# One layer of a GLA and Fourier diffusion backbone: a place of its own for a quarter of the folded h, fewer adaLN steps at GLA's end, slab products and turns in one run

## The chip, the cores and the metric

The kernel runs on one core of one Trainium2 chip. The metric is device time in microseconds of one execution, taken as the median of several runs. TensorE (PE) multiplies matrices, VectorE (DVE) and ScalarE (ACT) work on elements, GpSimd (POOL) fills and adds a little, and SyncE (SP) hands transfers to the DMA queue, in order. Each engine works through its own list of instructions and waits on counts that the others raise.

## The reference

One layer works on 384 tokens (128 of context, 256 latent) of width 2048, in fp32. Cut to what the change touches:

```python
mod = jax.nn.silu(cond) @ lw['w_ada'] + lw['b_ada']
sh1, sc1, ga1, sh2, sc2, ga2 = [m[:, None, :] for m in jnp.split(mod, N_MOD, axis=-1)]
h = rmsnorm(x, lw['norm_pre_mix']) * (1.0 + sc1) + sh1
m, s_f, s_b = mixer(h, s0_f, s0_b, n_chunks, lw)
x = x + ga1 * rmsnorm(m, lw['norm_post_mix'])
h = rmsnorm(x, lw['norm_pre_ffn']) * (1.0 + sc2) + sh2
ff = (jax.nn.silu(h @ lw['w_ffn_gate']) * (h @ lw['w_ffn_up'])) @ lw['w_ffn_down']
```

`cond` is one vector for latent and one for context tokens, so that `mod` has six parts (adaLN) of 2048 channels by 2. The mixer projects h with `w_in` into q, k, v, output gate, low-rank decay factors and Fourier channels; it runs a chunked gated linear attention (GLA) in both directions, a 2-D DFT over tokens and channels of each Fourier group, and merges the two with sigmoid gates `h @ w_gate`; `w_out` follows, and then a dense feed-forward layer.

## The kernel before, in words

All activations lie turned: 128 channels on the partitions, 384 tokens along the free dimension, 16 such tiles (`KT`). An fp32 product is made of three matmuls of a rounded part and a remainder of each factor (`passes`: A_hi with whi, A_hi with wlo, A_lo with whi). ACT rounds a raw weight tile to whi (L256, and L394 for the narrow tile of w_x), DVE subtracts to get wlo (L257, L395). For h they are A_hi (ACT, L331) and A_lo (DVE, L332).

**First stage** (loop from L521 over the 16 channel tiles). For tile kb, `gemv(kb)` multiplies silu(cond) with a 2 MB slab of w_ada (two 1 MB transfers, 16 fp32 matmuls per tile) into columns 0 to 255 of a PSUM tile `pgm`; ACT copies them (`ev`, L562), two PE transposes turn them into columns 256 to 511 of the same tile (L568), DVE reduces these (L575) to shift and scale (`mods`, L576 and L580) and applies them to the normalised x, which gives h (`scr`, L582). From h come A_hi and A_lo. The projection to v runs one tile behind: `vprod(kb - 1)` in three runs of six matmuls (pv, L462). Two further projections (`xprod`, px, L480) and, every fourth tile, the low-rank product of four tiles (`lrprod`, px, L487) share one PSUM tile `px`; after each of them DVE adds px to its sum (`flush`, L475), before the next may start. `todo` holds these px products of an iteration in order: the first runs ahead of the turns, the second behind them, the third behind the second run of pv, the fourth at the end. DVE's subtractions for the next weights (`lag`) come behind A_lo, and then the parts of h's fold for the Fourier branch (`fold_h`, L424 and L426). SP's queue carries slabs (pool of five 1 MB tiles), raw tiles of w_v and xraw tiles of w_x (two of each). The folded h is written to DRAM (`hf_d`).

**adaLN's other blocks.** The five half blocks of parts 2, 3, 4 are formed on DVE by a generator, two half steps of adacc (L664) per 512 KB of weights. `meted` takes as many of them per step of the main loop as `rate` says; while GLA runs, its generator `gla()` yields that number at each of its own steps, and 2 is used once it has ended. A finished block is brought together on PE (pr, L674), copied by ACT (L638) and turned (ptm, L642). The half block left over is made on PE (`ada_pe`, pr from adax, L699) in the stage of `w_out`, where the rest of the DVE generator is used up at tile 12.

**Fold.** Behind GLA the folded h is read back in four quarters (`fetch`, L983) into the two buffers of `fx`. For each quarter `parts_of` makes four fp32 matmuls (bnp, L999), whose weights wn DVE forms once (L992), and splits the quarter into xe and xo. `xo` takes the place of the tiles B_hi and B_lo. The quarters run as steps between the units of the gates.

Of the kernel before, what the change touches and what calls it, by code (L numbers as in the profile page):

```python
# [11 lines left out]
F32 = mybir.dt.float32  # L12
# [11 lines left out]
KT = D // P  # L24
# [83 lines left out]
def tile_step(ctx: ExitStack, tc: tile.TileContext, a, o):  # L108
    nc = tc.nc
    PE, ACT, DVE, POOL, SP = nc.tensor, nc.scalar, nc.vector, nc.gpsimd, nc.sync  # L110
# [34 lines left out]
    def alloc_r(t, name):  # L145
        return tuple(actp.tile([P, 8, T], F32R, tag=f"{t}_{n}", name=f"{name}_{n}") for n in ("hi", "lo"))
# [183 lines left out]
    def split_act(hi, lo, src):  # L330
        ACT.copy(hi, src)  # L331
        DVE.tensor_sub(lo, src, hi.bitcast(F32))  # L332
# [28 lines left out]
    hf_d = dram.tile([P, KT, T], F32, name="hf_d")  # L361
# [3 lines left out]
    with ExitStack() as s:  # L365
# [6 lines left out]
        def load_slab(kb):  # L372
            slabs[kb] = [pb.tile([P, KT // 2, 256], F32, tag="slab", name="slab", bufs=5) for _ in range(2)]
            for n, sl in enumerate(slabs[kb]):
                SP.dma_start(sl, a["w_ada1"][kb, :, n * (KT // 2) : (n + 1) * (KT // 2), :])
# [3 lines left out]
        def load_w(kb):  # L379
            load()  # L380
            xraw[kb] = pb.tile([P, XU * P], F32, tag="xraw", name="xraw", bufs=2)
            SP.dma_start(xraw[kb], a["w_x"][kb])
# [47 lines left out]
        def keep_h(q):  # L430
            (ACT if q else SP).dma_start(hf_d[:, 8 * q : 8 * q + 8, :], xnt[q])
# [9 lines left out]
        def gemv(kb, ks=range(KT)):  # L441
            slab = slabs[kb]
            for k in ks:
                q = 32 * (k % 4)
                PE.matmul(  # L445
                    pgv[q : q + 32, :], spad[:, k, :], slab[k // (KT // 2)][:, k % (KT // 2), :],
                    start=k < 4, stop=k >= KT - 4,
                )

        def passes(w):  # L450
            return ((0, w[0]), (0, w[1]), (1, w[0]))
# [19 lines left out]
        def flush(acc, first, dst=None):  # L471
            if first:
                DVE.tensor_copy(acc, px)
            else:
                DVE.tensor_add(dst if dst is not None else acc, acc, px)  # L475

        def xprod(u, kb, w):
            def mm():
                for j, (x_, w_) in enumerate(passes(w)):
                    PE.matmul(px, w_[:, u * P : (u + 1) * P], hT[x_][:, kb, :], start=j == 0, stop=j == 2)  # L480

            return mm, lambda dst=None: flush(xacc[u], kb == 0, dst)

        def lrprod(kb):
            def mm():
                for q in range(4):
                    PE.matmul(  # L487
                        px[32 * q : 32 * q + 32, :], wlr[:, kb + q, :], scr[:, (kb + q) % 8, :], start=True, stop=True,
                    )

            return mm, lambda dst=None: flush(lracc, kb == 0, dst)
# [30 lines left out]
        prev = None  # L522
        for kb in range(KT):
            if kb and kb + 1 < KT:
                load_slab(kb + 1)
                load_w(kb + 1)
                if kb == 4:
                    load_later()

            if kb == KT - 1:  # L530
                load()
                pre = pb.tile([P, KT // 2, 256], F32, tag="slab", name="pre", bufs=5).rearrange("p a b -> p (a b)")
                for n in range(2):
                    load(pre[:, G * n : G * n + G])
            wait = kb in (1, 2)
            if kb and not wait:
                gemv(kb)
            todo = []
            if kb > 4 and kb % 4 == 2:
                todo.append(lrprod(kb - 6))  # L540
            if kb:
                todo += [xprod(u, kb - 1, prev[1]) for u in range(XU)]
            todo += [None] * (4 - len(todo))
            flushes = [t[1] if t else lambda: None for t in todo]

            def pe_x(n):
                if todo[n]:
                    todo[n][0]()

            if wait:  # L550
                vprod(kb - 1, prev[0], (0,))
            pe_x(0)
            hf = scr[:, kb % 8, :]

            xr = hf if kb else qs[0]
            DVE.tensor_mul(xr, xn(kb), rstd if kb else px)
            flushes[0]()
            if wait:
                gemv(kb)
            if kb:  # L560
                ev = pb.tile([P, 256], F32, tag="ev", name="ev")
                ACT.copy(ev, pgv)  # L562
            lag = []
            new = split_w(kb, lag)
            if kb:
                vprod(kb - 1, prev[0], (1 if wait else 0,))
            for m in range(2):
                PE.transpose(pmod[:, m, :], ev[:, m * P : (m + 1) * P], ident)  # L568
            pm = pb.tile([P, 2, 2], F32, tag="pm", name="pm")
            if kb == 0:  # L570

                for _ in range(6):
                    PE.matmul(pv[5][:, 0:P], ones, ones, start=True, stop=True)
            pe_x(1)
            DVE.tensor_reduce(pm, bands, axis=mybir.AxisListType.X, op=ALU.add)  # L575
            DVE.tensor_scalar(  # L576
                mods[:, 1, kb, :], pm[:, 1, :], bsc1[:, 0, kb : kb + 1], norms[:, 0, kb : kb + 1],
                op0=ALU.add, op1=ALU.mult,
            )
            DVE.tensor_scalar_add(mods[:, 0, kb, :], pm[:, 0, :], cols[:, 0, kb : kb + 1])  # L580
            for lo, hi, c in segs:
                DVE.tensor_scalar(  # L582
                    hf[:, lo:hi], xr[:, lo:hi], mods[:, 1, kb, c : c + 1], mods[:, 0, kb, c : c + 1],
                    op0=ALU.mult, op1=ALU.add,
                )
                if kb == 0:
                    ACT.activation(
                        hT[0][:, kb, lo:hi], xr[:, lo:hi], AF.Identity,
                        bias=mods[:, 0, kb, c : c + 1], scale=mods[:, 1, kb, c : c + 1],
                    )  # L590
            flushes[1]()
            if kb:
                split_act(hT[0][:, kb, :], hT[1][:, kb, :], hf)
            else:
                ACT.copy(rstd, px)
                DVE.tensor_sub(hT[1][:, kb, :], hf, hT[0][:, kb, :].bitcast(F32))
            if kb:
                if not wait:
                    vprod(kb - 1, prev[0], (1,))
                pe_x(2)  # L600
                flushes[2]()
            for sub in lag:
                sub()
            fold_h(kb)
            if kb == KT - 2:
                keep_h(0)
            if kb:
                vprod(kb - 1, prev[0], (2,))
                pe_x(3)
                flushes[3]()  # L610
            prev = new
# [97 lines left out]
    def on(t, h):  # L709

        return qk[:, h:8:4, t * P : (t + 1) * P]
# [16 lines left out]
    with ExitStack() as s:  # L728
# [9 lines left out]
        for c in range(2):  # L738
            src = a["a2"][:, 512 * c : 512 * c + 512]
# [17 lines left out]
        def gla():  # L757
# [10 lines left out]
            for h in range(NH):  # L768
# [129 lines left out]
                for d in range(2):  # L898
                    for n in range(2):
                        t = n * (1 + d)  # L900
# [26 lines left out]
            for t in range(3):  # L927
                for h in range(NH):
                    z = on(t, h)
                    ACT.mul(z, z, rs[:, t, h : h + 1])  # L930
                yield 2

        def keep(t, i):
            return lambda p: ACT.copy(t[:, i, :], p)
# [34 lines left out]
    with ExitStack() as s:  # L969
# [9 lines left out]
        fold_in.append(pxe)  # L979
        fx = actp.tile([P, 2, 4, T], F32, tag="C_lo", name="fx")  # L980

        def fetch(b):
            SP.dma_start(fx[:, b % 2], hf_d[:, 4 * b : 4 * b + 4, :])  # L983

        fetch(0)
        fetch(1)
        xe = pxe.tile([P, KT, 2, HT], F32R, name="xe")
        xo = alloc_r("B", "xo")
        wn4 = pxe.tile([P, G], F32, tag="ws", name="wn4")[:, 0 : 32 * KT].rearrange("p (k c) -> p k c", c=32)
        POOL.memset(wn4, 0.0)  # L990
        w01 = wnr.rearrange("p (g i) k -> p i k g", i=2)
# [2 lines left out]

        def parts_of(b):

            src = fx[:, b % 2]
            for q in range(4):
                PE.matmul(  # L999
                    bnp[32 * q : 32 * q + 32, :], wn4[:, 4 * b + q, :], src[:, q, 0:HT], start=b == 0, stop=b == 3,  # L1000
                )
            e = xe[:, 4 * b : 4 * b + 4]
            split_act(e[:, :, 0], e[:, :, 1], src[:, :, 0:HT])
            d = xo[b // 2][:, 4 * (b % 2) : 4 * (b % 2) + 4]
            split_act(d[:, :, 0:HO], d[:, :, HO : 2 * HO], src[:, :, HT:T])
            if b < 2:
                fetch(b + 2)

        def folding():
            for b in range(4):  # L1010
# [228 lines left out]
    with ExitStack() as s:  # L1239
# [675 lines left out]
        for kind, c, i in steps:  # L1915
# [14 lines left out]
            if kind == "D":  # L1930
                w = grab2()
                n, kh = i // 2, i % 2
                if kh == 0:
# [8 lines left out]
                todo = [  # L1942
                    (pd_tiles[t], [[x[:, 2 * kh + m, t * P : (t + 1) * P] for m in range(2)] for x in h], mov_d, kh == 0, kh == 1)
                    for t in ts
                ]
# [24 lines left out]
            elif kind[0] == "D":  # L1970
# [3 lines left out]
                todo = []  # L1974
# [8 lines left out]
            else:  # L1983
# [4 lines left out]
                B = banks(c)  # L1988
# [232 lines left out]
```

## Time and profile before

| | |
|---|---|
| time, median of 3 runs | 1919.46 us (1918.77 to 1920.14) |
| profiled execution, time | 1918.24 us |
| profiled execution, span | 1916.5 us |
| TensorE clock granted, mean | 0.999 |
| PE busy | 1894.8 us (99%) |
| DVE busy | 1637.8 us (85%) |
| ACT busy | 1081.0 us (56%) |
| DMA moved | 435.65 MB, mean 227 GB/s |

The profile is of one execution; the span is from its first to its last instruction, and its time has what lies around these besides. In a row of a timeline stand start, duration, engine, line, operation, out<-in and shape, the count of instructions, and in square brackets the idle time just before it with what ended that. A duration counts until the result is there, so that successive matmuls overlap; the rate of PE is read from one start to the next. PEld are weight loads, which run beside the matmuls. SPq and PEq are the queues' own instructions.

### The profile page before, as it was taken

Reading aid. Unit: us, or ns where it says so; the run is one execution under the profiler, and the core shown is the slowest. Engines: PE = TensorE matmul, PEld = TensorE weight load, DVE = VectorE, ACT = ScalarE, POOL = GpSimd, SP = SyncE. Lnnn points to the kernel's source line nnn. Section 1 sums busy time; section 2 is a strip of 40 time slices with the busy share of each in tenths; the row PEclk is TensorE's granted clock in tenths of the full one; section 3 lists DMA queues with packets and bytes.
Section 4 is the critical chain, followed back from the end, with each engine's and each line's share of the span. In section 5 each row is a group of like instructions: output and inputs, shape, how many; then the busy total and the mean of one; then the engine's idle time right before and its main releaser. Section 6 shows DMA issues by size and latency. Waiting matters only on the chain.

```text
span 1916.5 us, 27971 instructions
## 1 busy us (share of the span) xinstructions
PE 1894.8 (99%) x10364; PEld 1669.1 (87%) x10364; DVE 1637.8 (85%) x2120; ACT 1081.0 (56%) x1569; POOL 160.8 (8%) x189
## 2 busy tenths in 40 slices
PE   8999999999999999999999999999999999999997
PEld 5779999999999999999988888888888888888886
DVE  6777989787867897877799999999999999988985
ACT  4335545554447554446457666766676666666554
POOL 0000001000000000004000111111102021111001
PEclk9999999999999999999999999999999999999999
DMA  9986777786765788766449697888879696959563
GB/s 390 376 328 201 236 236 229 237 281 207 228 193 189 259 272 286 285 216 217 145 144 273 167 250 185 240 205 222 214 209 240 183 249 175 270 126 271 135 221 101
DMA packets 247385, 435.65 MB, mean 227 GB/s; under 512 B 45772, under 2 KB 150412, under 8 KB 242640
## 3 DMA queue, kind: packets, MB, share of 16 engines
q1 hardware_dynamic: 199648, 391.59, 60.8%
q0 software_dynamic: 18944, 33.63, 11.5%
q10 hardware_dynamic: 28656, 8.65, 2.5%
q8 instruction: 81, 1.33, 0.3%
q14 instruction: 56, 0.46, 0.1%
HBM read 369.05 MB, written 57.67 MB: 223 GB/s over the span
## 4 chain that ended last, share of the span: by engine, by line
PE 85%; DVE 6%; DMA 4%; ACT 2%; issue 1%; SPq 0%; DVEq 0%; ACTq 0%
PE pgu L1737 31%; PE pmm L291 25%; PE pdn L1737 10%; PE pds L1737 7%; PE pv L462 3%; DVE wlo L257 1%; PE pfo L1100 1%; PE pgm L445 1%; DVE adacc L664 1%; PE pmm L1451 1%; ACT whi L256 1%; PE px L480 1%; PE pfo L1101 1%; PE bk L1737 1%; DMA xraw<-in_w_x 1%
## 5 line engine op out<-in xcount | busy, mean ns | idle before, releaser
L291 PE MATMUL pmm<-A_hi,whi 128*128 128x384 f32 x1072 | 361.9, 338 | 0.0
L291 PE MATMUL pmm<-A_lo,whi 128*128 128x384 f32 x1072 | 358.7, 335 | 0.0
L291 PE MATMUL pmm<-A_hi,wlo 128*128 128x384 f32 x1072 | 358.7, 335 | 0.0
L1635 ACT CAST whi<-u 128x1024 fp32r<-128x1024 f32 x200 | 210.7, 1055 | 174.7 <-PE pgu L1737 40.9
L1646 DVE TENSOR_TENSOR wlo<-u,whi 128x1024 fp32r<-128x1024 f32 x200 | 244.2, 1223 | 34.8 <-ACT whi L1635 30.4
L256 ACT CAST whi<-raw 128x1024 fp32r<-128x1024 f32 x163 | 171.1, 1053 | 158.2 <-DMA raw<-in_w_out 59.0
L1737 PE MATMUL pgu<-whi,A_hi 128*128 128x512 f32 x640 | 249.9, 390 | 0.0
L1737 PE MATMUL pgu<-whi,A_lo 128*128 128x512 f32 x640 | 249.1, 389 | 0.0
L257 DVE TENSOR_TENSOR wlo<-raw,whi 128x1024 fp32r<-128x1024 f32 x161 | 196.1, 1221 | 42.4 <-ACT whi L256 41.7
L1635 ACT CAST whi<-raw 128x1024 fp32r<-128x1024 f32 x157 | 165.2, 1054 | 84.9 <-PE pgu L1737 25.3
L291 PEld LDWEIGHTS pmm<-A_hi,whi 128*128 128x128 f32 x1072 | 201.2, 188 | 5.5 <-issue 4.1
L291 PEld LDWEIGHTS pmm<-A_lo,whi 128*128 128x128 f32 x1072 | 201.4, 188 | 0.5 <-DVE A_lo L332 0.2
L291 PEld LDWEIGHTS pmm<-A_hi,wlo 128*128 128x128 f32 x1072 | 201.2, 188 | 0.0
L1646 DVE TENSOR_TENSOR wlo<-raw,whi 128x1024 fp32r<-128x1024 f32 x157 | 191.8, 1222 | 11.0 <-ACT whi L1635 10.5
L664 DVE SCALAR_TENSOR_TENSOR adacc<-adaw,cond,adacc 128x1024 f32<-128x1024 f32 x150 | 186.8, 1281 | 14.5 <-DMA adaw<-in_w_ada 14.2
L1737 PE MATMUL pgu<-wlo,A_hi 128*128 128x512 f32 x640 | 185.8, 389 | 0.0
L1737 PEld LDWEIGHTS pgu<-whi,A_hi 128*128 128x128 f32 x640 | 120.1, 188 | 25.9 <-issue 0.8
L1737 PEld LDWEIGHTS pgu<-wlo,A_hi 128*128 128x128 f32 x640 | 120.1, 188 | 25.1
L1737 PEld LDWEIGHTS pgu<-whi,A_lo 128*128 128x128 f32 x640 | 120.1, 188 | 24.8
L1737 PE MATMUL pgu<-whi,S 128*128 128x512 f32 x400 | 116.6, 389 | 0.0
L1870 POOL DMA_DIRECT2D sums_d<-spare x64 | 58.5, 954 | 622.6 <-ACT spare L1866 601.4
L1737 PE MATMUL pdn<-whi,hid_hi 128*128 128x512 f32 x264 | 102.8, 389 | 0.0
(466 smaller groups left out, 3536.1 us busy)
## 6 DMA issues: line engine op xcount, KB each, us to landing
adaw<-in_w_ada SPq DMA_DIRECT2D x80, 512.0 KB, 4.6
raw<-in_w_d SPq DMA_DIRECT2D x70, 512.0 KB, 6.0
slab<-in_w_ada SPq DMA_DIRECT2D x32, 1024.0 KB, 11.3
raw<-in_w_gate SPq DMA_DIRECT2D x64, 512.0 KB, 4.3
raw<-in_w_g SPq DMA_DIRECT2D x48, 512.0 KB, 3.8
raw<-in_w_u SPq DMA_DIRECT2D x48, 512.0 KB, 5.1
u<-in_w_u SPq DMA_DIRECT2D x40, 512.0 KB, 5.5
u<-in_w_g SPq DMA_DIRECT2D x40, 512.0 KB, 9.5
```

What stands on the lines that cost most here:

```text
L256: ACT.copy(hi, raw)
L257: sub = lambda: eng.tensor_sub(lo, raw, hi.bitcast(F32))
L291: PE.matmul(dst, w[wi][:, k * n + n0 : k * n + n0 + P], x[xi][:, k0 + k, :], start=first and k == 0 and j == 0, stop=last and k == kts - 1 ...
L445: PE.matmul(pgv[q : q + 32, :], spad[:, k, :], slab[k // (KT // 2)][:, k % (KT // 2), :], start=k < 4, stop=k >= KT - 4,)
L462: PE.matmul(pv[2 * t + g], hT[x_][:, kb, t * P : (t + 1) * P], w_[:, g * 512 : (g + 1) * 512], start=kb == 0 and j == 0, stop=kb == KT - 1 ...
L480: PE.matmul(px, w_[:, u * P : (u + 1) * P], hT[x_][:, kb, :], start=j == 0, stop=j == 2)
L664: DVE.scalar_tensor_tensor(acc[:, c, :], w, cond[:, k, c : c + 1], acc[:, c, :], op0=ALU.mult, op1=ALU.add,)
L1100: PE.matmul(p, w[0][:, c], x[:, 0 : 2 * n], start=kh == k == 0, stop=False)
L1635: ACT.copy(hi, src)
L1646: DVE.tensor_sub(lo, src, hi.bitcast(F32))
L1737: PE.matmul(dst, stat[x_][m], mov(w[w_], m), start=first and w_ == m == x_ == 0, stop=last and w_ == m == 1, skip_group_check=any(more),)
L1870: POOL.dma_start(sums_d[k], u, accum_op=ALU.add)
```

## The change

It has three parts.

In the first stage, `joined` holds for tiles 6 to 15. There `gemv(kb + 1)` is written right behind the two turns of tile kb; gemv(6) stays at the head of its iteration. The low-rank product of a joined tile is put second in `todo` instead of first. From tile 6 on a slab is asked for one tile earlier than the w tiles: slab 8 behind gemv(7), slab 9 ahead of w 8, and so on.

In GLA, the last three steps yield 2, 1 and 0 instead of 2, 2 and 2.

In the fold, quarter 2 goes into the half of `xo` that takes the place of B_lo's channels 4 to 7, and is asked for together with quarters 0 and 1; quarter 3 goes into `fx[:, 0]` and is asked for behind part 0.

```diff
--- before.py
+++ after.py
@@ -522,7 +522,10 @@
         prev = None
         for kb in range(KT):
             if kb and kb + 1 < KT:
-                load_slab(kb + 1)
+                if kb < 7:
+                    load_slab(kb + 1)
+                elif kb + 2 < KT:
+                    load_slab(kb + 2)
                 load_w(kb + 1)
                 if kb == 4:
                     load_later()
@@ -533,13 +536,17 @@
                 for n in range(2):
                     load(pre[:, G * n : G * n + G])
             wait = kb in (1, 2)
-            if kb and not wait:
+            joined = kb > 5
+            if kb and not wait and kb < 7:
                 gemv(kb)
             todo = []
-            if kb > 4 and kb % 4 == 2:
+            low = kb > 4 and kb % 4 == 2
+            if low and not joined:
                 todo.append(lrprod(kb - 6))
             if kb:
                 todo += [xprod(u, kb - 1, prev[1]) for u in range(XU)]
+            if low and joined:
+                todo.insert(1, lrprod(kb - 6))
             todo += [None] * (4 - len(todo))
             flushes = [t[1] if t else lambda: None for t in todo]
 
@@ -566,6 +573,10 @@
                 vprod(kb - 1, prev[0], (1 if wait else 0,))
             for m in range(2):
                 PE.transpose(pmod[:, m, :], ev[:, m * P : (m + 1) * P], ident)
+            if joined and kb < KT - 1:
+                gemv(kb + 1)
+                if kb == 6:
+                    load_slab(kb + 2)
             pm = pb.tile([P, 2, 2], F32, tag="pm", name="pm")
             if kb == 0:
 
@@ -928,7 +939,7 @@
                 for h in range(NH):
                     z = on(t, h)
                     ACT.mul(z, z, rs[:, t, h : h + 1])
-                yield 2
+                yield 2 - t
 
         def keep(t, i):
             return lambda p: ACT.copy(t[:, i, :], p)
@@ -979,13 +990,15 @@
         fold_in.append(pxe)
         fx = actp.tile([P, 2, 4, T], F32, tag="C_lo", name="fx")
 
+        xo = alloc_r("B", "xo")
+        folded = [fx[:, 0], fx[:, 1], xo[1][:, 4:8, :].bitcast(F32), fx[:, 0]]
+
         def fetch(b):
-            SP.dma_start(fx[:, b % 2], hf_d[:, 4 * b : 4 * b + 4, :])
-
-        fetch(0)
-        fetch(1)
+            SP.dma_start(folded[b], hf_d[:, 4 * b : 4 * b + 4, :])
+
+        for b in range(3):
+            fetch(b)
         xe = pxe.tile([P, KT, 2, HT], F32R, name="xe")
-        xo = alloc_r("B", "xo")
         wn4 = pxe.tile([P, G], F32, tag="ws", name="wn4")[:, 0 : 32 * KT].rearrange("p (k c) -> p k c", c=32)
         POOL.memset(wn4, 0.0)
         w01 = wnr.rearrange("p (g i) k -> p i k g", i=2)
@@ -994,7 +1007,7 @@
 
         def parts_of(b):
 
-            src = fx[:, b % 2]
+            src = folded[b]
             for q in range(4):
                 PE.matmul(
                     bnp[32 * q : 32 * q + 32, :], wn4[:, 4 * b + q, :], src[:, q, 0:HT], start=b == 0, stop=b == 3,
@@ -1003,8 +1016,8 @@
             split_act(e[:, :, 0], e[:, :, 1], src[:, :, 0:HT])
             d = xo[b // 2][:, 4 * (b % 2) : 4 * (b % 2) + 4]
             split_act(d[:, :, 0:HO], d[:, :, HO : 2 * HO], src[:, :, HT:T])
-            if b < 2:
-                fetch(b + 2)
+            if b == 0:
+                fetch(3)
 
         def folding():
             for b in range(4):
```

On PE, in the first stage round tile 8 (pgm from slab are the slab products, pgm from ident the turns), this stood before, from one tile's slab products to the next's:

```order
L445 MATMUL pgm<-slab,spad 32x256 x16
L480 MATMUL px<-A_hi,whi 128x384
L480 MATMUL px<-A_hi,wlo 128x384
L480 MATMUL px<-A_lo,whi 128x384
L462 MATMUL pv<-whi,A_hi 128x512 x6
L568 MATMUL pgm<-ident,ev 128x128 x2
L480 MATMUL px<-A_hi,whi 128x384
L480 MATMUL px<-A_hi,wlo 128x384
L480 MATMUL px<-A_lo,whi 128x384
L462 MATMUL pv<-wlo,A_hi 128x512 x6
L462 MATMUL pv<-whi,A_lo 128x512 x6
```

After the change it reads:

```order
L480 MATMUL px<-A_hi,whi 128x384
L480 MATMUL px<-A_hi,wlo 128x384
L480 MATMUL px<-A_lo,whi 128x384
L462 MATMUL pv<-whi,A_hi 128x512 x6
L575 MATMUL pgm<-ident,ev 128x128 x2
L445 MATMUL pgm<-slab,spad 32x256 x16
L480 MATMUL px<-A_hi,whi 128x384
L480 MATMUL px<-A_hi,wlo 128x384
L480 MATMUL px<-A_lo,whi 128x384
L462 MATMUL pv<-wlo,A_hi 128x512 x6
L462 MATMUL pv<-whi,A_lo 128x512 x6
```

The 16 slab products moved from ahead of the tile's first px to behind its turns, and belong to the next tile there. DVE's own list between them is the same in both, from the reduction to the fold of h:

```order
L586 TENSOR_REDUCE pm<-pgm 128x4
L587 TENSOR_SCALAR mods<-pm,bsc_82,norms 128x2
L591 TENSOR_SCALAR mods<-pm,cols_b 128x2
L593 TENSOR_SCALAR scr<-scr,mods 128x128
L593 TENSOR_SCALAR scr<-scr,mods 128x256
L475 TENSOR_TENSOR xacc_141<-xacc_141,px 128x384
L332 TENSOR_TENSOR A_lo<-scr,A_hi 128x384
L257 TENSOR_TENSOR wlo<-raw,whi 128x1024
L395 TENSOR_TENSOR wlo<-xraw,whi 128x256
```

These are rows of the changed kernel; in the kernel before they stand in this order with L575, L576, L580 and L582. In both, the reduction waits for PE's count; what raises that count now is not the turns but the products behind them.

On PE in the stage of `w_out`, tile 12, before the change adaLN's last blocks stood so between the matmuls of the tiles (pmm):

```order
L674 MATMUL pr<-adacc,selr 32x256 x8
L699 MATMUL pr<-adax,cpad 32x256 x16
L291 MATMUL pmm<-A_hi,whi 128x384
L291 MATMUL pmm<-A_lo,whi 128x384
L291 MATMUL pmm<-A_hi,wlo 128x384
...
L642 MATMUL ptm<-ident,adacc 128x128 x2
L642 MATMUL ptm<-ident,evp 128x128 x2
```

And so after it:

```order
L710 MATMUL pr<-adax,cpad 32x256 x16
L291 MATMUL pmm<-A_hi,whi 128x384
L291 MATMUL pmm<-A_lo,whi 128x384
L291 MATMUL pmm<-A_hi,wlo 128x384
...
L685 MATMUL pr<-adacc,selr 32x256 x8
L653 MATMUL ptm<-ident,evp 128x128 x2
L653 MATMUL ptm<-ident,adacc 128x128 x2
```

The products of the DVE block (pr from adacc) moved from ahead of 24 matmuls to behind them, and stand next to the turns that use them.

## The prediction

> **What bounds the kernel now.** I read the page first, then a table of engine time by stretch, then PE's waits by releaser, then the timeline of the three places the change touches.
>
> ```profile
> span 1916.5 us, 27971 instructions
> PE 1894.8 (99%) x10364; PEld 1669.1 (87%) x10364; DVE 1637.8 (85%) x2120; ACT 1081.0 (56%) x1569; POOL 160.8 (8%) x189
> ...
> 0.00:64.00 64.00, 57.76 (x421) 38.56 (x422) 40.02 (x109) 26.82 (x62) 1.35 (x9) 1.00 0.98 385
> 64.00:144.00 80.00, 79.86 (x593) 57.57 (x592) 59.43 (x158) 25.96 (x65) 0.00 (x0) 1.00 0.91 348
> ```
>
> The columns of the last two rows are window, length, then busy us of PE, PEld, DVE, ACT, POOL, the clock granted, the DMA share and GB/s. TensorE (PE) is the bound: 1894.8 of 1916.5 us, at full clock. From 64 to 144 us, where the first stage is edited, it is idle for 0.14 us of 80: an edit there can win only the little that changing from one kind of matmul to another costs, and whatever makes PE wait is lost in full. At the fold PE waits twice, 0.92 and 0.81 (rows below), and that is all that can be won there.
>
> **The change part by part. 1: the first stage, tiles 6 to 14.** This is one tile of it now, from its slab products (pgm, L445) to the next tile's:
>
> ```profile
> 76.29 1.93 PE L445 MATMUL pgm<-slab,spad 128*32 128x256 f32 x32
> 78.15 0.44 PE L480 MATMUL px<-A_hi,whi 128*128 128x384 f32 x1
> 78.34 0.37 ACT L562 COPY ev<-pgm 128x256 f32<-128x256 f32 x1 [3.06 <-PE pgm L445]
> 78.78 1.55 PE L462 MATMUL pv<-whi,A_hi 128*128 128x512 f32 x6
> 80.17 0.38 PE L568 MATMUL pgm<-ident,ev 128*128 128x128 f32 x2
> 80.30 0.42 PE L480 MATMUL px<-A_hi,whi 128*128 128x384 f32 x1
> 80.65 0.17 DVE L575 TENSOR_REDUCE pm<-pgm 128x4 f32<-128x16 f32 x1 [1.12 <-PE pgm L568]
> 80.91 1.55 PE L462 MATMUL pv<-wlo,A_hi 128*128 128x512 f32 x6
> 83.75 1.50 PE L445 MATMUL pgm<-slab,spad 128*32 128x256 f32 x24
> 84.18 0.42 DVE L395 TENSOR_TENSOR wlo<-xraw,whi 128x256 fp32r<-128x256 f32 x1
> ```
>
> A tile takes 83.75 − 76.29 = 7.46 us. By starts on PE: slab products 1.86 (to 78.15), px 0.63, pv 1.39, the two turns (L568) 0.13, px 0.61, and two runs of pv for the rest. Moving the products behind the turns adds and removes no matmul. What it moves is a release. In the program as changed the turns no longer raise PE's count; the next count stands at the end of the slab products behind them, and VectorE's (DVE's) reduction waits for that one. Now it starts 0.48 after the turns (80.17 → 80.65). After, it starts after 0.13 to 0.20 for the turns plus the 2.05 that pass from the first product to the engine that waits for the last (76.29 → 78.34): some 2.2 after the turns. DVE then runs its list in order, reduction, mods, scr, flush of px, A_lo, wlo, and reaches the subtraction wlo (L395) 84.18 − 80.65 = 3.53 later. The next tile's first px needs that wlo in its second matmul. Such a wait is in the trace, in the tiles before 6:
>
> ```profile
> 22.21 0.42 DVE L395 TENSOR_TENSOR wlo<-xraw,whi 128x256 fp32r<-128x256 f32 x1
> ...
> 22.68 0.45 PE L480 MATMUL px<-A_hi,wlo 128*128 128x384 f32 x1 [0.72 <-DVE wlo L395]
> ...
> 39.47 0.45 PE L480 MATMUL px<-A_hi,wlo 128*128 128x384 f32 x1
> ...
> 39.93 1.31 PE L462 MATMUL pv<-whi,A_hi 128*128 128x512 f32 x5
> ```
>
> From the subtraction's start to that matmul 0.47, from it to pv 0.46 (39.47 → 39.93), pv 1.39, and the next turns follow. From turns to turns: 0.17 + 2.05 + 3.53 + 0.47 + 0.46 + 1.39 = **8.07 us, where 7.46 stood**. PE's own work would fill only 0.13 + 1.86 + 0.61 + 3 × 1.39 + 0.63 = 7.40 (or 7.31, if fewer switches save 0.09), so DVE's chain sets the pace, by 0.67.
>
> Three of the nine intervals also hold the low-rank product (px, L487; tiles 6, 10, 14). These are the turns of tiles 6 and 15, and rows round tile 10:
>
> ```profile
> 64.37 0.38 PE L568 MATMUL pgm<-ident,ev 128*128 128x128 f32 x2
> ...
> 92.98 0.83 PE L487 MATMUL px<-scr,wlr 128*32 128x384 f32 x8
> 93.73 1.66 PE L462 MATMUL pv<-whi,A_hi 128*128 128x512 f32 x6
> ...
> 97.57 0.45 PE L480 MATMUL px<-A_hi,whi 128*128 128x384 f32 x1
> ...
> 98.41 0.56 DVE L475 TENSOR_TENSOR xacc<-xacc,px 128x384 f32<-128x384 f32 x1 [0.21 <-PE px L480]
> 98.88 1.22 DVE L257 TENSOR_TENSOR wlo<-raw,whi 128x1024 fp32r<-128x1024 f32 x1
> 100.01 0.42 DVE L395 TENSOR_TENSOR wlo<-xraw,whi 128x256 fp32r<-128x256 f32 x1
> ...
> 134.43 0.38 PE L568 MATMUL pgm<-ident,ev 128*128 128x128 f32 x2
> ```
>
> After the change the low-rank product stands behind the slab products, so xprod's second unit starts 0.13 + 1.86 + 0.75 (92.98 → 93.73) + 1.39 = 4.13 after the turns; its flush on DVE 0.84 later (97.57 → 98.41), wlo of the large tile 0.47 after that, L395 another 1.13, then 0.47 + 0.46 + 1.39 as above: 8.89. From the turns of tile 6 (64.37) to those of tile 15 (134.43) is 70.06 us. After: 3 × 8.89 + 6 × 8.07 = 75.1, so +5.0. The low bound of this term is PE's own 9 × (7.40 − 7.46) = −0.5, and −1.5 with the 0.09 per tile and the wait behind the low-rank flush (0.2 us in one row) won as well. I take the chain: every link of it is measured, and nothing in DVE's list is moved out of its way.
>
> **The slab of tile 7** is now wanted behind the turns of tile 6, at 64.4 (its second half at 65.3), not at 68.83, and is not asked for any earlier:
>
> ```profile
> 52.38 8.81 DMA slab<-in_w_ada
> ...
> 60.42 0.33 SPq L214 DMA_DIRECT2D raw<-in_w_v  x1
> ...
> raw<-in_w_v SPq DMA_DIRECT2D x3, 512.0 KB, 8.7
> ...
> 68.83 1.93 PE L445 MATMUL pgm<-slab,spad 128*32 128x256 f32 x32
> ```
>
> The DMA engines are 98% busy at 385 GB/s there. The second half of slab 6 lands at 52.38 + 8.81 = 61.19. Behind it in SP's queue stand 0.66 MB of w and 2.10 MB of slab 7: 2.75 MB / 385 GB/s = 7.2 us, landing 68.4. From the other side: the raw tile asked for at 60.42 lands 8.7 later, 69.1, and is 0.66 MB (1.7 us) behind slab 7: 67.4. Between them 67.9, so **+2.6** (65.3 → 67.9). Bounds: nothing, and 4.4 (products that started at 68.83 waited for nothing, so their second half lay there by 69.7). The following slabs are asked for a tile ahead of w, 2.75 MB per 8.07 us is 341 GB/s, under the 385 that flow, so I put no wait on them.
>
> On DMA the Trainium skill ("DMA: Bandwidth & Descriptors", Where 436 GB/s comes from) gives 435 GB/s as the ceiling of the SBUF ports. At that rate the 2.75 MB would take 6.3 us and not 7.2, and the stall would be an estimated 0.9 shorter. This trace shows 385 at a 98% share, and the measurement decides.
>
> **2: the fold.** Quarter 2 of h gets a place of its own and quarter 3 is asked for behind part 0 instead of part 1:
>
> ```profile
> 415.30 2.48 DVE L664 SCALAR_TENSOR_TENSOR adacc<-adaw,cond,adacc 128x1024 f32<-128x1024 f32 x2
> 417.69 0.26 DVE L992 TENSOR_TENSOR wn<-wnr 128x64 f32<-128x64 f32 x1
> 418.16 0.54 PE L999 MATMUL bnp<-fx,wn 128*32 128x194 f32 x8 [0.92 <-ACT xe L331]
> 420.90 0.33 SPq L983 DMA_DIRECT2D fx<-hf_d  x1
> 426.34 0.33 SPq L983 DMA_DIRECT2D fx<-hf_d  x1
> 433.57 0.54 PE L999 MATMUL bnp<-fx,wn 128*32 128x194 f32 x8 [0.81 <-DMA fx<-hf_d]
> ```
>
> Asked for at 420.90 instead of 426.34, 5.4 earlier, quarter 3 is there long before 433.57: **−0.8**. The other wait, at 418.16, is put down to ACT, but wn itself ends only at 417.95 on DVE, behind two half steps of adacc (415.30 to 417.69). Two half steps stand right before wn in the changed order too, because the rate is 2 again once the generator has ended; I take −0 there, bound −0.9.
>
> **3: fewer half steps.** The three last steps of GLA take 2, 1, 0 half steps instead of 2, 2, 2. None is dropped, so DVE's 3 × 1.24 move on behind matmuls that leave DVE room (59.43 of 80 us busy in one stretch, 85% over all). But the last block of adaLN ends one half tile later, in the w_out stage. There its products (pr) now follow the 24 matmuls instead of preceding them, and its turning (ptm) needs ScalarE's copy of pr right away:
>
> ```profile
> 836.59 0.33 PE L291 MATMUL pmm<-A_hi,wlo 128*128 128x384 f32 x1
> ...
> 838.11 0.53 ACT L1262 ACTIVATE sq<-Blo 128x384 f32<-128x384 f32 x1
> ...
> 841.01 1.07 PE L674 MATMUL pr<-adacc,selr 128*32 128x256 f32 x16
> ...
> 842.15 0.37 ACT L638 COPY adacc<-pr 128x256 f32<-128x256 f32 x1 [0.74 <-PE pr L674]
> ```
>
> ACT has a tile's own four operations to do first, until 838.64, 2.05 after the tile's last matmul starts; with the copy and its signal some 2.4. PE meanwhile has one matmul (0.33), pr (1.07 busy, overlapping it) and the other turning, about 1.3. **+1.1**, bounds 0 and 1.7.
>
> **Sum.** +5.0 + 2.6 − 0.15 (tile 6 loses its low-rank product before its turns) − 0.8 + 1.1 = +7.8. The profiled execution's own 1918.24 becomes 1926.0; it lies 1.2 under the median of 1919.46, so on the medians **1927.3 us**.
>
> **The rivals.** *A, the release is as early as now* and PE sets the pace: first stage −1.5 and −0.15, fold −0.8, w_out +1.1: 1918.1, or 1917.0 without the last. It decides if the reduction starts less than 1.5 us after the turns. For it: nothing in the data makes the reduction need the products. Against: the count it waits for. *B, the chain, but slab 7 in time*: 1924.7. For it: the 67.4 and 68.4 are worked out, not seen. *C, the chain is covered* (px not reached before wlo) and slab 7 alone costs: −0.5 + 2.6 − 0.8 − 0.15 + 1.1 = +2.3, 1921.7. Against: 8.07 is over 7.40 by more than any link could be off. *D, DVE's later chain also meets late loads* (slab order puts w8 behind slab 9): 5.0 + 4.4 − 0.15 − 0.8 + 1.7 is +10.2, 1929.6.
>
> The reduction reads columns 256 to 511 of the tile into whose columns 0 to 255 the products are written. The Trainium skill ("PSUM — Partial Sum Buffer", PSUM bank collisions raise a hardware error) says that two engines may not be in one bank and quadrant at once, even at different addresses. By that rule A could not run as I put it, and its chance would go to the forecast, with the sum as it stands; no run here shows it, since in this trace PE has always left pgm when DVE reads it.
>
> **How the numbers follow.** Forecast 0.53, B 0.2, D 0.05, C 0.1, A 0.12. What a measurement of this kernel can tell from no change is 0.2%, 3.8 us: slower is over 1923.3, faster under 1915.6. Forecast, B and D lie above: slower 0.78. C and most of A are the same: 0.17. Faster needs A and the 0.9 of the wait at wn and more: 0.05. The likeliest case's own range is 1923.5 (no stall at slab or w_out) to 1929.6 (D); C is taken in below, A left out: the range is 1920 to 1930.
>
> **What would show it.** In the changed profile: the reduction about 2.2 us after the turns' start; a wait of px for wlo (L395) in each of tiles 7 to 15, some 0.5 to 0.7 each; one wait of pgm for the slab's DMA near 64 to 68; turns 8.1 and 8.9 apart; no wait of bnp for DMA; and a wait of ptm for ACT near 843. I am wrong if the reduction starts before the products have ended, or if the px rows carry no wait.

## The result, and the profile after

The changed kernel takes 1928.81 us (median of 6 runs, 1926.55 to 1932.85); the kernel before, beside it, 1919.8 us (6 runs, 1918.11 to 1922.31). The ratio is 1.0047, 95% interval 1.0035 to 1.0059: **0.47% slower, some 9 us**. The forecast was 1927.3, in a range of 1920 to 1930. The profiled execution is the longest of the changed kernel's six, 1932.85 us; its 13 us over before are thus more than the change's own share, and this section says which part is.

The changed kernel's page, then the row of engine time for the stretch of the first stage (columns as before), then PE's waits by releaser (total us, times, longest):

```profile
span 1931.1 us, 27979 instructions
PE 1899.9 (98%) x10364; PEld 1670.8 (87%) x10364; DVE 1636.7 (85%) x2120; ACT 1078.6 (56%) x1569; POOL 160.4 (8%) x189
```

```profile
64.00:144.00 80.00, 74.30 (x559) 52.04 (x558) 51.76 (x145) 21.96 (x58) 0.00 (x0) 1.00 0.83 324
```

```profile
PE px L480 <- DVE wlo L395: 5.5, 11, 0.7
...
PE pmm L291 <- ACT whi L256: 1.7, 1, 1.7
PE px L1068 <- DVE fs L1118: 1.5, 1, 1.5
PE pmm L291 <- DVE A_lo L332: 1.3, 1, 1.3
PE pgm L445 <- DMA slab<-in_w_ada: 1.3, 2, 1.1
PE bnp L1012 <- issue: 1.2, 1, 1.2
...
PE ptm L653 <- ACT adacc L649: 0.7, 1, 0.7
```

PE was busy for 79.86 us of the 80 between 64 and 144; now for 74.30. That is where most of the time went: 5.7 us of idle PE in one stretch. One tile of the first stage, in the changed kernel's timeline:

```profile
82.34 0.38 PE L575 MATMUL pgm<-ident,ev 128*128 128x128 f32 x2
82.65 1.93 PE L445 MATMUL pgm<-slab,spad 128*32 128x256 f32 x32
...
84.72 0.17 DVE L586 TENSOR_REDUCE pm<-pgm 128x4 f32<-128x16 f32 x1 [2.68 <-PE pgm L445]
...
88.25 0.42 DVE L395 TENSOR_TENSOR wlo<-xraw,whi 128x256 fp32r<-128x256 f32 x1
...
88.72 0.45 PE L480 MATMUL px<-A_hi,wlo 128*128 128x384 f32 x1 [0.48 <-DVE wlo L395]
89.18 1.55 PE L462 MATMUL pv<-whi,A_hi 128*128 128x512 f32 x6
90.58 0.38 PE L575 MATMUL pgm<-ident,ev 128*128 128x128 f32 x2
```

DVE stands idle for 2.68 us and is released by the slab products (L445), no longer by the turns. The reduction starts 2.38 behind the turns (0.48 before), L395 3.53 after it, the px that needs it 0.47 later, pv 0.46, the turns 1.40: 8.24 from turns to turns. PE's wait row shows 0.48 of the loss; the interval shows all of it, 0.78 over 7.46.

```profile
63.81 0.38 PE L575 MATMUL pgm<-ident,ev 128*128 128x128 f32 x2
64.12 1.07 PE L445 MATMUL pgm<-slab,spad 128*32 128x256 f32 x16
66.31 1.07 PE L445 MATMUL pgm<-slab,spad 128*32 128x256 f32 x16 [1.12 <-DMA slab<-in_w_ada]
...
98.81 0.38 PE L575 MATMUL pgm<-ident,ev 128*128 128x128 f32 x2
...
107.79 0.38 PE L575 MATMUL pgm<-ident,ev 128*128 128x128 f32 x2
...
141.46 0.38 PE L575 MATMUL pgm<-ident,ev 128*128 128x128 f32 x2
```

The turns of tiles 6 and 15 stand 141.46 − 63.81 = 77.65 apart (70.06 before), +7.6, with slab 7's second half waited for once. The turns of tile 6 come 0.56 sooner (64.37 → 63.81), so that everything behind the first stage is 7.0 later. Some 0.4 of the 0.56 is no gain of the change: tile 6 takes 8.11 in this one execution of before, but 7.60 in fold_alone and yield_alone, whose first stage is the same, and 7.47 here. Against those two the stage costs 7.5.

Followed by PE's marks (when each matmul starts in both profiles), the delay is 7.0 up to 396 us, 6.4 behind the fold's four bnp, 8.2 behind the wait for fs at 472, and 13.4 from 873 on. The part between 640 and 760 us, up to 4 of these, is waits for weights (pmm for whi or A_lo) that come in other sizes in the runs below, also in those without GLA's edit (1.6 and 1.6 in subtract_first_from_8_fold), so that I do not count them to the change. That the change has no part in them is not shown: from 640 to 800 us the six profiles with GLA's edit or a piece of it lose 1.4 to 4.1 against this one of before (2.7 in the mean), the seven without it −0.1 to 3.5 (1.4). The rest, 7.0 − 0.6 + 1.8 and 1.1 behind ptm at 861, is 9.3, or 9.8 with the 7.5: both lie in what the runs' times say, 9.0 (6.7 to 11.3).

### The profile page after: what moved, and what is told of

Read it like the earlier page. It is cut to its first block, busy times and chain, and to the rows that moved or that the text cites. A ratio compares the mean times of both kernels' runs of the same rounds, so it can differ in the third digit from the quotient of the medians.

```text
span 1931.1 us, 27979 instructions
## 1 busy us (share of the span) xinstructions
PE 1899.9 (98%) x10364; PEld 1670.8 (87%) x10364; DVE 1636.7 (85%) x2120; ACT 1078.6 (56%) x1569; POOL 160.4 (8%) x189
## 4 chain that ended last, share of the span: by engine, by line
PE 84%; DVE 7%; DMA 5%; ACT 3%; issue 2%; SPq 0%; DVEq 0%; ACTq 0%
PE pgu L1750 31%; PE pmm L291 24%; PE pdn L1750 10%; PE pds L1750 7%; PE pv L462 2%; DVE wlo L257 2%; DMA adaw<-in_w_ada 1%; PE pgm L445 1%; DVE adacc L675 1%; ACT whi L256 1%; PE pfo L1113 1%; PE pmm L1464 1%; PE px L480 1%; DMA slab<-in_w_ada 1%; PE bk L1750 1%
```

## The experiments

Each was timed in turn with the kernel before. The ratio stands with its 95% interval; it is not simply the quotient of the two medians shown.

| run | what of the change it holds | median us | before us | ratio |
|---|---|---|---|---|
| join_alone | first stage | 1926.26 | 1919.28 | 1.0039 (1.0025 to 1.0053) |
| fold_alone | fold | 1918.33 | 1919.28 | 0.9992 (0.9984 to 1.0000) |
| yield_alone | GLA's end | 1921.09 | 1919.28 | 1.0013 (1.0003 to 1.0022) |
| products_behind_px | first stage, one line moved | 1922.12 | 1919.28 | 1.0015 (1.0005 to 1.0024) |
| join_subtract_first | first stage, wlo ahead of the reduction | 1920.77 | 1919.75 | 1.0012 (1.0002 to 1.0022) |
| join_from_8 | first stage from tile 8 | 1925.57 | 1919.75 | 1.0031 (1.0020 to 1.0043) |
| subtract_first_from_8_fold | both of these, and the fold | 1918.28 | 1919.75 | 0.9992 (0.9983 to 1.0001) |
| half_steps_rate_2 | GLA's end, and a faster rate later | 1924.72 | 1919.75 | 1.0026 (1.0015 to 1.0036) |
| behind_px_low_rank_first | as products_behind_px, low-rank first | 1923.58 | 1919.74 | 1.0020 (1.0010 to 1.0030) |
| half_steps_2_1_1 | GLA's end with 2, 1, 1 | 1919.96 | 1919.74 | 1.0001 (0.9992 to 1.0009) |
| half_steps_2_2_1 | GLA's end with 2, 2, 1 | 1921.00 | 1919.74 | 1.0005 (0.9996 to 1.0013) |
| one_step_made_up | GLA's end, one step made up | 1919.82 | 1919.74 | 1.0001 (0.9992 to 1.0009) |

### The three parts apart

Each of these three holds one part of the diff above and nothing of the other two: the hunks of the first stage, those of `fetch` and `parts_of`, and the one line `yield 2 - t`.

> The first stage's edit alone (products behind the turns, low-rank product second, slabs a tile earlier); fold and GLA's end as before. Chain theory: the turns of tiles 6 and 15 stand 77.6 us apart as in the changed kernel's profile (70.06 before), PE waits for wlo (L395) about 0.5 us in each of nine tiles, and the time is 7.0 us over before's. Rival (half steps and fold make the loss, the first stage is covered later): under 2 us. Rival (the late loads of the later stages follow from the first stage's delay): 9 us or more, with waits for loads behind 450 us.

> The fold's edit alone. Expected: bnp's wait for DMA (0.81) gone, the wait at wn kept, -0.8 us, which is inside what can be told. If the earlier quarter pushes other loads, a new wait for a load behind 396 us and no gain.

> GLA's last three steps alone with 2, 1, 0 half steps. Theory formed on the changed kernel's profile: the three half steps come back in the fold, where adaw is not asked for ahead, DVE waits there for its load, fs comes late and PE waits 1.5 for it; and in the w_out stage ptm waits 0.7 for ACT: +1 to +3 us. Rival (those waits belong to the first stage's delay or to that one execution): 0, and neither wait in the profile.

The ratios are +0.39%, −0.08% and +0.13%; their sum, 0.44%, is close to the whole change's 0.47%. The first stage carries the loss. The eleven waits for wlo (two of them are in before too) are in join_alone's profile as in the changed kernel's, but the turns of tiles 6 and 15 stand 80.26 apart there and not the 77.6 expected: slab 7 is waited for twice, 2.1 us in all, and PE is slow for some 3 us behind it (last section).

```profile
PE px L480 <- DVE wlo L395: 5.5, 11, 0.7
```

fold_alone's profile has no wait of bnp for DMA left, as expected. The wait at wn stayed, 1.5 us in that execution against 0.92 before, so that less than 0.81 shows there. The gain is on the edge of what can be told. In yield_alone the wait for fs, which I had not forecast, and that of ptm, which I had, are there without the first stage's edit:

```profile
PE px L1055 <- DVE fs L1105: 1.4, 1, 1.4
...
PE ptm L642 <- ACT adacc L638: 0.7, 1, 0.7
```

One wait is missing from yield_alone's profile: that of bnp for DMA, which the fold's edit was made for. It is in all six profiles that hold neither the fold's edit nor GLA's (0.3 to 1.9 us), and in none of the five that hold GLA's, whole or in part, without the fold's; yield_alone's four bnp stand 4.8 apart. So either part takes this wait away, and the change can win it only once. Why GLA's edit does it was not tried.

### What in the first stage makes the loss

`products_behind_px` joins the same tiles, with the same order of slabs, but writes the products one place later, so that they stand behind the reduction:

```diff
-            if joined and kb < KT - 1:
-                gemv(kb + 1)
-                if kb == 6:
-                    load_slab(kb + 2)
...
             pe_x(1)
             DVE.tensor_reduce(pm, bands, axis=mybir.AxisListType.X, op=ALU.add)
+            if joined and kb < KT - 1:
+                gemv(kb + 1)
+                if kb == 6:
+                    load_slab(kb + 2)
```

> The first stage's edit with one line moved: the slab products stand behind the px that follows the turns, and behind the reduction in the order of the text, so that the reduction waits for the turns alone; slab order, low-rank place and the early demand for slab 7 stay. Fold and GLA's end as before. Chain theory: reduction 0.5 us behind the turns again, no wait for wlo, tile 7.4 to 7.6 us, what is left is the slab of tile 7 (0.5 to 1.3 us): +0.5 to +2 us. Rival (the order of slabs and w makes the loss): about as much as the joined stage alone, +7.

```profile
82.42 0.38 PE L575 MATMUL pgm<-ident,ev 128*128 128x128 f32 x2
...
82.90 0.17 DVE L582 TENSOR_REDUCE pm<-pgm 128x4 f32<-128x16 f32 x1 [1.12 <-PE pgm L575]
...
83.26 1.93 PE L445 MATMUL pgm<-slab,spad 128*32 128x256 f32 x32
...
89.91 0.38 PE L575 MATMUL pgm<-ident,ev 128*128 128x128 f32 x2
...
97.42 0.38 PE L575 MATMUL pgm<-ident,ev 128*128 128x128 f32 x2
...
106.39 0.38 PE L575 MATMUL pgm<-ident,ev 128*128 128x128 f32 x2
```

The reduction is released by the turns again, 0.48 behind them, and the tile takes 89.91 − 82.42 = 7.49. The order of slabs and w, the same in both runs, is not the cause. But the measured +0.15%, 2.8 us, is more than the +0.5 to +2 expected (its interval begins at 1.0): the interval behind a tile with the low-rank product is still 106.39 − 97.42 = 8.97, with a wait for wlo in it (8.33 in before).

I put that on the low-rank product's new place, and moved it back:

```diff
-            if low and not joined:
+            if low:
                 todo.append(lrprod(kb - 6))
...
-            if low and joined:
-                todo.insert(1, lrprod(kb - 6))
```

> As the run with the slab products behind px, and the low-rank product first in its iteration again. Chain theory: there the three intervals behind tiles 6, 10, 14 were still 8.95 because the second flush of px stands ahead of wlo; with the low-rank product first they go back to 8.3, no wait for wlo is left in the joined tiles, and only slab 7 (1.3) and the switches remain: +1 to +1.5 us against +2.8. If the place of the low-rank product does not matter: +2.8.

This was wrong: +0.20%. These rows stand behind tile 10.

```profile
97.93 0.38 PE L573 MATMUL pgm<-ident,ev 128*128 128x128 f32 x2
...
104.94 0.44 PE L480 MATMUL px<-A_hi,wlo 128*128 128x384 f32 x1 [0.56 <-DVE wlo L395]
...
106.78 0.38 PE L573 MATMUL pgm<-ident,ev 128*128 128x128 f32 x2
```

8.85, close to the 8.97 of the run above, and the same again behind tile 14. A tile with three px products has its last one behind the second run of pv, and the slab products push that run 1.87 later wherever the low-rank product stands. Its flush comes later on DVE, and wlo stands behind the flush. So the place of the low-rank product is not the cause, and what is left is DVE's order. That is what `join_subtract_first` changes alone in the joined stage, with the reduction left waiting for the products:

```diff
             pe_x(1)
+            if joined:
+                for sub in lag:
+                    sub()
+                lag = []
             DVE.tensor_reduce(pm, bands, axis=mybir.AxisListType.X, op=ALU.add)
```

> The first stage's edit as it is, but in the joined tiles DVE subtracts both wlo (L257, L395) ahead of the reduction, where it stands idle for 2.7 us, and not behind A_lo. The reduction still waits for the products. Chain theory: the chain from the reduction to L395 is off PE's path, the nine waits for wlo go, turns 7.5 us apart and some 8.3 with the low-rank product, slab 7 still waits for 1.1 to 1.4: +1 to +3 us in all. Rival (PE itself is slower in the joined order, by its switches): no change from the joined stage, +7.

```profile
81.70 1.22 DVE L257 TENSOR_TENSOR wlo<-raw,whi 128x1024 fp32r<-128x1024 f32 x1 [0.23 <-ACT whi L256]
82.84 0.42 DVE L395 TENSOR_TENSOR wlo<-xraw,whi 128x256 fp32r<-128x256 f32 x1
84.43 0.17 DVE L590 TENSOR_REDUCE pm<-pgm 128x4 f32<-128x16 f32 x1 [1.17 <-PE pgm L445]
...
82.11 0.38 PE L575 MATMUL pgm<-ident,ev 128*128 128x128 f32 x2
82.42 1.93 PE L445 MATMUL pgm<-slab,spad 128*32 128x256 f32 x32
...
89.59 0.38 PE L575 MATMUL pgm<-ident,ev 128*128 128x128 f32 x2
```

The reduction is as late as in the changed kernel (2.32 behind the turns), DVE uses the gap for the two subtractions, and the tile takes 7.48. Round a low-rank product the two intervals are 7.49 and 8.16, where before had 7.60 and 8.33. The nine waits for wlo are gone, and of join_alone's +0.39% there is left +0.12%, where slab 7 still waits (2.1 us in two rows). This settles the first stage: **not the late reduction in itself, but wlo behind it in DVE's list** costs, and PE's own work in an ordinary tile of the joined order is no shorter than it was (7.48 and 7.46).

`join_from_8` begins the joined tiles two later (`kb > 7`, and the other bounds with it):

> The first stage's edit alone, begun two tiles later (joined from tile 8, not 6; slab 9 behind the turns of tile 8). Chain theory: two intervals go back to their old length (0.65 + 0.76) and the next wanted slab is nearer to its place, so that its wait goes (1.1 to 1.4): +4 to +5 us. If the slab still waits, +5.5; if the loss hung on slab 7 alone, under +1.

+0.31%, 6 us, with an interval (3.8 to 8.3) that holds the +4 to +5 expected. In its profile the turns of tiles 6 and 15 stand 74.89 apart, 4.8 over before's. No wait for a slab is left in the stage: that wait belongs to the one tile whose slab is wanted earlier than it was asked for.

`subtract_first_from_8_fold` puts the later begin and the early subtractions together with the fold's edit.

> A version to beat both: joined from tile 8, both subtractions ahead of the reduction, and the fold's edit; GLA's end as before. Chain theory: joined tiles at 7.5 for 7.46, three quarters of a microsecond won at the fold: -1 to +1 us, no difference that can be told. If joining wins its switches after all, -2.

0.9992 (0.9983 to 1.0001), the same as the fold's edit alone. From tile 6 to tile 15 it takes 69.5 us in its profile, 0.5 less than before, won round the low-rank products of tiles 10 and 14. No version here beats the kernel before by more than can be told.

### What GLA's last steps do

The three half steps moved on meet two places. For the first, the fold, I had two theories, and moved on two and one half steps instead of three (`yield (2, 1, 1)[t]` and `yield (2, 2, 1)[t]` for `yield 2 - t`):

> GLA's last steps with 2, 1, 1 half steps (two moved on, not three). Two theories of PE's wait for fs in the fold (1.4 with three moved on): (a) an odd number splits the pairs, so that a step of two takes the second half of one load and the first of the next and waits for it: with an even number the wait for adaw goes and fs waits 0 to 0.5; (b) the half steps that now stand ahead of fs are the cost, whatever their pairing: 0.6 to 1.2. The wait of ptm for ACT stays (0.7) in both, since the last block still ends behind the 24 matmuls. Time +1 to +2 us.

> GLA's last steps with 2, 2, 1 half steps (one moved on). By (a), pairing: DVE waits for adaw inside its steps of the fold as with three, and fs keeps PE waiting about 1. By (b), the work ahead of fs: one half step less than with 2, 1, 1, and PE's wait for fs is the least of the three, 0 to 0.5. The wait of ptm stays. Time +0.5 to +2 us.

These are DVE's rows ahead of fs with three (yield_alone), two and one moved on:

```profile
443.52 1.28 DVE L664 SCALAR_TENSOR_TENSOR adacc<-adaw,cond,adacc 128x1024 f32<-128x1024 f32 x1
446.93 1.28 DVE L664 SCALAR_TENSOR_TENSOR adacc<-adaw,cond,adacc 128x1024 f32<-128x1024 f32 x1 [2.13 <-DMA adaw<-in_w_ada]
...
460.16 2.48 DVE L664 SCALAR_TENSOR_TENSOR adacc<-adaw,cond,adacc 128x1024 f32<-128x1024 f32 x2 [1.27 <-DMA adaw<-in_w_ada]
...
463.69 0.62 DVE L1105 TENSOR_TENSOR fs<-fs,pfo 128x194 f32<-128x194 f32 x2
```

```profile
452.56 2.47 DVE L664 SCALAR_TENSOR_TENSOR adacc<-adaw,cond,adacc 128x1024 f32<-128x1024 f32 x2
456.08 2.48 DVE L664 SCALAR_TENSOR_TENSOR adacc<-adaw,cond,adacc 128x1024 f32<-128x1024 f32 x2
459.62 0.61 DVE L1105 TENSOR_TENSOR fs<-fs,pfo 128x194 f32<-128x194 f32 x2
```

```profile
443.37 1.27 DVE L664 SCALAR_TENSOR_TENSOR adacc<-adaw,cond,adacc 128x1024 f32<-128x1024 f32 x1
447.10 1.28 DVE L664 SCALAR_TENSOR_TENSOR adacc<-adaw,cond,adacc 128x1024 f32<-128x1024 f32 x1 [2.45 <-DMA adaw<-in_w_ada]
...
460.11 0.61 DVE L1105 TENSOR_TENSOR fs<-fs,pfo 128x194 f32<-128x194 f32 x2
```

An odd number does split the pairs: DVE waits 2.13 and 2.45 for adaw inside a step of two, and not at all with an even number. But PE waits for fs only with three: 0.4 to 1.5 us in the four profiles that have that edit. Neither theory holds alone: (a) wanted a wait with one moved on, (b) 0.6 to 1.2 with two. What delays fs to 463.69 is both together, three half steps ahead of it and waits for adaw among them; with less of either, this row of fs starts by 460.1. Neither is told apart from before by its time (1.0001 and 1.0005): the first lies under the +1 to +2 us expected of it, the second within its +0.5 to +2, and the wait of ptm (0.7) is in both profiles, as expected.

The second place is the stage of w_out. One more step of the generator behind tile 11 brings its last block forward again:

```diff
                 step(ada)
                 step(by_pe)
+            if i == KT - 5:
+                step(ada)
             if i == KT - 4:
```

> GLA's last steps with 2, 1, 0 half steps, and one more step of the adaLN generator at the end of tile 11 of the w_out stage, so that its last block ends where it did and its products stand ahead of the 24 matmuls again. Theory: the wait of ptm for ACT goes and 1.1 us with it; the wait for fs stays: +0.7 us against +1.8. If the wait of ptm is covered elsewhere, no change.

The wait of ptm for ACT is gone from the profile, and the ratio falls from 1.0013 to 1.0001. That is about the 1.1 us expected and, in this run, a shorter wait for fs too (0.4 against 1.4), so the two are not told apart by the time. half_steps_2_1_1, which keeps the wait of ptm, runs as fast (1.0001), so that no time here shows what that wait is worth.

`half_steps_rate_2` tried the same by `rate[0] = 2` for 1.6 in that stage:

> GLA's last three steps with 2, 1, 0 half steps, and 2 instead of 1.6 half steps per half tile in the w_out stage, so that the last DVE block is ready before tile 12 again; first stage and fold as before. Theory: the waits at the end of that stage (ptm for ACT 0.7, pr for adacc 0.3) go, the wait of px for fs (1.4) stays: +0.8 us against +1.8 with 1.6. If all of the loss comes from the w_out stage: 0. If more half steps crowd DVE there: over +1.8, with waits of pmm for wlo.

It lost more, +0.26% (its interval still meets that of yield_alone), and not as any of the three theories had it. The last block now ends in mid-stage, its ptm again right behind 24 matmuls that follow its pr, and PE's one wait there is longer: ahead of the tile's own operations ACT rounds a raw tile of w_out, for which it had itself waited 2.16 us on DMA. These are rows of windows in that stretch (length, busy us of PE, PEld, DVE, ACT, POOL, clock, DMA share, GB/s):

```profile
836.00:839.00 3.00, 1.13 (x8) 0.81 (x6) 1.87 (x3) 2.84 (x6) 0.00 (x0) 1.00 0.56 175
839.00:842.00 3.00, 3.00 (x13) 3.00 (x14) 2.85 (x7) 1.05 (x1) 0.00 (x0) 0.69 0.83 242
842.00:845.00 3.00, 3.00 (x15) 3.00 (x15) 1.41 (x3) 1.04 (x1) 0.00 (x0) 0.74 0.98 336
845.00:848.00 3.00, 3.00 (x19) 3.00 (x18) 2.20 (x5) 2.57 (x5) 0.00 (x0) 1.00 0.80 300
```

PE waits 1.9 us for ACT, and then the clock granted falls: 0.69 and 0.74 over six microseconds, 13 and 15 matmuls where 19 go at full clock. Eleven matmuls from 840.12 on take 3.47 us, where they would take 1.9 at 0.17 each: the wait has cost some 1.5 us more than its own length.

## Why the prediction was right, point by point

**Where it lay.** 1927.3 forecast, 1928.81 measured; +7.8 forecast, +9.0 measured (interval of the ratio: 6.7 to 11.3). The likeliest case was the one that came.

**The release** was right: the reduction 2.38 behind the turns, forecast 2.2; L395 3.53 later, forecast 3.53; waits of px of 0.48 to 0.56 in nine tiles, forecast 0.5 to 0.7. The two runs that take the chain away by different links (the release; wlo's place behind it) both bring the ordinary tile back to 7.5.

**The interval was undersized**: 8.07 forecast, 8.23 measured, and 8.98 for 8.89 behind the low-rank product. The link that failed is the 0.13 to 0.20 for the turns. Turns to slab products takes 0.31 (82.34 → 82.65), where turns to px takes 0.13. Over nine intervals the chain costs 77.65 − 1.3 − 70.06 = +6.3, and not +5.0.

**The slab of tile 7 was oversized**: 1.12 and not 2.6 in the changed kernel, 1.3 with the interval's own length taken off (10.31 − 8.98). It landed at 66.26 and not 67.9. In join_alone and join_subtract_first its waits add up to 2.1. The 0.15 for tile 6 was right: 7.47 for the 7.60 of fold_alone and yield_alone. So the chain's +1.3 and the slab's −1.3 cancel, and the stage costs some 7.5, forecast +7.45. That the sum came out so well is in part luck.

**The fold**: its wait for DMA went, as forecast (0.81 in the trace of before, none with the edit; all four bnp stand 4.8 apart). The wait at wn stayed, 1.2 in the changed kernel for 0.92. But the forecast gave the 0.8 to the fold's edit alone, and GLA's edit takes the same wait away without it (the five profiles above).

**The half steps**: the wait of ptm was forecast at 1.1; the row of the waits says 0.7, and by PE's marks 1.1 are lost between ptm and the tile's next matmuls (12.3 late, then 13.5). The step that failed is "none is dropped, so they move on behind matmuls that leave DVE room": room over all was not room where they landed, ahead of fs, for whose lateness PE waited 1.5. The forecast put this at nothing, and it is as much as the forecast lacked (1.2).

**The rivals.** A (the release as early as now) and C (the chain covered) are refuted by the rows above; B and D by the slab's 1.1 and by the stage without any other wait of PE for a load. The Trainium skill's rule on PSUM ("PSUM — Partial Sum Buffer", PSUM bank collisions raise a hardware error) agrees with what was seen: in no run do DVE's reduction and PE's products to the other half of that tile overlap. No run tried to let them.

## What to carry to other kernels

A matmul that is moved behind another one into the same PSUM tile takes over the release of whoever reads the tile: count from the last write to the reader, and then down the reader's whole list to the next thing PE needs, since what stands behind the late instruction in that list is late too. That the shared tile does it shows in before: there px products, into a tile of their own, follow the turns on PE (80.30 to 81.07), and the reduction starts among them, at 80.65. A version with the slab products in a tile of their own was not run. If the engine that was made to wait has work that does not hang on the release, put that work ahead of the wait; here four lines did it, and won back most of the loss. Work that is only shifted in a paced generator has to be followed to the place where it lands, with the parity of its pairs and the loads they ask for.

## What the runs showed of the hardware

A short idle can cost more than its length. In half_steps_rate_2 a wait of 1.9 us was followed by some 3.3 us with matmuls 0.32 apart instead of 0.17, and in join_alone two waits for slab 7 (0.71 and 1.42, within 4 us) by these rows, which the changed kernel's execution with one wait of 1.12 does not have:

```profile
64.00:68.00 4.00, 1.87 (x23) 0.76 (x25) 0.00 (x0) 0.00 (x0) 0.00 (x0) 0.95 1.01 414
68.00:72.00 4.00, 4.00 (x29) 1.84 (x22) 2.13 (x7) 0.95 (x4) 0.00 (x0) 0.62 1.02 426
```

Tiles 6 to 7 took 12.97 us there (turns at 64.03 and 77.00) for 10.31. The Trainium skill ("TensorE: Matmul & The Clock Gate", What's actually happening) ties the drop to a window of about 3.4 us that runs freely; the length of the slow stretch agrees, but waits well below 3.4 us were enough. Whether a given wait sets it off differed: one of 1.9 us in one_step_made_up (pmm for whi) did not, and nor did the very same two waits in join_subtract_first, 0.70 and 1.43 at the same place, with PE as busy from 64 to 68 us (1.87) and the clock at 1.00 throughout:

```profile
67.66 1.07 PE L445 MATMUL pgm<-slab,spad 128*32 128x256 f32 x16 [1.43 <-DMA slab<-in_w_ada]
```

So the length of the idle time does not decide it alone. What else does, no run here shows.
